# The mixers' output product: pair differences on GpSimd instead of VectorE, and the last pair's operands formed ahead of the first product

## The chip, the cores and the metric

The kernel runs on one core of one Trainium2 chip. The metric is the device time of one execution in microseconds (us), the median of several runs. TensorE multiplies matrices into PSUM banks, VectorE and ScalarE do element-wise work and read PSUM, GpSimd works on SBUF only and issues transfers of its own queue, SyncE issues the other transfers. Every engine works through its own instructions in the order of the program.

## The reference, cut to what matters

One decoder layer on 512 tokens with 1024 channels: a half-step FFN, two parallel mixers (a convolution module and a dilated attention), a gated sum of both through one output matrix, a second half-step FFN, a per-layer embedding and a last norm. The change touches the output of the mixers:

```python
a = jax.nn.silu(layer_norm(a, g_ln, b_ln))
y_conv = a @ w_conv_out                       # unit "co": 8 column blocks of 128
y_attn = o.reshape(b, s, ATTN_OUT_W) @ w_attn_out
g_a, g_b = jnp.split(jax.nn.sigmoid(gate_logits), 2, axis=-1)
h = h + (g_a * y_conv + g_b * y_attn) @ w_mix_out
h = h + 0.5 * swiglu(rms_norm(h, g_ffn2), w_ffn2_gate, w_ffn2_up, w_ffn2_down)
```

## The kernel before

Activations lie channel by token in tiles of 128x512 floats. Every float operand of a product is split into a high and a low half (a ScalarE copy in reduced precision makes the high one, a VectorE subtraction the low one), and a product is three matmuls: high by high, low by high, high by low.

The output matrix of the mixers is multiplied in a scheme with seven products instead of eight (`MIXED`: B11, T1, T2, B22, T3, B21, T4). Its eight input tiles are the gated sums `sg` of channel blocks 0 to 7. They form four pairs, block m with block m+4; each half is 256 tokens wide. `form_pair` queues the operands of a pair: differences of halves (`sub`, L638), ScalarE copies (`first_`, L650) and VectorE subtractions for the low halves (`end`, L653). Its parameter `by` names the engine of the differences. The two FFNs take the default (GpSimd); the mixers' output passes `BY`, which is VectorE before.

The stage that the change touches runs like this:

- The loop over m = 0 to 7 (L1519 on) runs `unit(p, ("co", m), cv)`, 24 matmuls of 128x512, then up to `N_FORM` = 10 queued steps of the pair of the turn before, then a multiplication by the gate (L1526, reads PSUM), the addition of the attention half (L1527), and the call of `form_pair` for this m. For m below 4 that queues five steps, one difference among them (T1's). For m from 4 on it queues ten: the difference t2, the copies for B21 with B22 and for T2, the low half of B21 with B22, two more differences, the low half of T2, the copy and the low half of T3 with T4, and a clean-up.
- So the ten steps of the last pair (m = 7, queued when the loop is over) are left for the products. `slab` fetches the weights of a product and, in the same call, prepares weights for products two or more ahead: a ScalarE copy (L401) and a VectorE subtraction (L402), each 128x1024, or weight sums on VectorE (L316 to L339), or the POOL transfers that form a low half by accumulation (L371, L373).
- In `for q in MIXED` (group g = 0, then g = 1) each product takes its slab, waits in the program for the operands that it needs, runs 24 matmuls of 128x256 in each half (`quarters_of`, L707, L708, L710), and `add` (L722, L725) adds the bank to the residual. Then `AFTER_M` says how many queued steps follow.
- B11, T2, T3 and T4 go to one PSUM bank (`pa`), T1 and B22 to `pd`, B21 to `pe`. A product accumulates on what its predecessor left in the bank, so the matmuls of T2 may start only when the addition of B11 has read `pa`, and those of B22 only when the addition of T1 has read `pd`.

On VectorE the order before is thus: gate and sum of block 7, the weight subtraction for T2, the addition of B11, t2, the low half of B21 with B22, the weight subtraction for B22, the addition of T1, two differences, the low half of T2.

Of the kernel before, what the change touches and what calls it, by code (L numbers as in the profile page):

```python
# [73 lines left out]

PLAN = (("gu", 2), ("gu", 3), ("gu", 4), ("gu", 5), ("dn", 1, 0), ("dn", 1, 1), ("gu", 6), ("gu", 7), ("gu", 8),
        ("dn", 2, 0), ("dn", 2, 1), ("gu", 9), ("gu", 10), ("dp", 0), ("dn", 3, 0), ("dn", 3, 1))
BY_ = False
N_FORM = 10
AFTER_M = {"B11": 4, "T1": 4, "T2": 3, "B22": 2, "T3": 2, "B21": 2, "T4": 2}
AFTER = {"B11": 1, "B21": 1, "T2": 1, "T1": 1, "T3": 2, "B22": 2}  # L80
TABLES = {"B21": 1, "T3": 1, "B22": 1, "T1": 1}
TABLES_P = 1
# [72 lines left out]
def block_kernel(ctx: ExitStack, tc: tile.TileContext, a, out):  # L155
# [208 lines left out]
    def spend(a_=0.0, v=0.0):  # L364
        spent[0] += a_
        spent[1] += v
# [242 lines left out]
    jobs, later = [], []  # L609
# [5 lines left out]
    def next_job(queue=None):  # L615
        f, a_, v = (queue or jobs or later).pop(0)
        if queue is not later:
            spend(a_, v)
        f()
# [368 lines left out]
    def into(v, xs, norm, resid):  # L988
        seen = []

        def first_(m):
            xs[m] = split(resid[m], "xs", gain(v, m))

        def second(m):
            norm.add(resid[m])
            seen.append(m)
            if len(seen) == KD:
                norm.flush()
        return first_, second
# [477 lines left out]
    def side(n):  # L1477
        if not bg:
            if lns:
                lns.pop(0)()  # L1480
        else:
            background(n)
# [33 lines left out]
    while lns:  # L1516
        side(0)
    BY = G if BY_ else V
    mixes, begun = [{} for _ in range(4)], []  # L1519
# [12 lines left out]
    begun = None  # L1532
    t = None
    cv.clear()
    xs, norm = [None] * KD, Norm()
    nxt2 = into(V_G2, xs, norm, h)
    for g in range(2):
        ps = {q: bank(q) for q in ("pa", "pe", "pd")}
        for q in MIXED:
# [8 lines left out]
            if g == 0:  # L1548
                for _ in range(min(AFTER_M.get(q, 0), len(later))):
                    next_job(later)  # L1550
# [4 lines left out]
            if g:  # L1555
                for _ in range(4 if q in ("B21", "T4") else min(AFTER_M.get(q, 0), len(later))):
                    next_job(later)
# [170 lines left out]
```

## Time and profile before

| | |
|---|---|
| median of 3 runs | 1286.78 us (1285.67 to 1287.22) |
| profiled execution, its own time | 1285.89 us |
| span of that execution | 1284.0 us |
| TensorE busy | 1269.0 us, 99% of the span |
| VectorE, ScalarE, GpSimd busy | 1017.2, 741.8, 300.8 us |
| granted TensorE clock | 0.998 of full speed, mean over the span |

A busy share tells little in so full a kernel. What matters is which engine TensorE waits for, and where; the rows of the section below show one stretch of some 30 us around the end of the loop over m, and the places elsewhere in the trace where GpSimd forms the same differences.

### The profile page before, as it was taken

To read this page: it belongs to the slowest core of one execution; us is meant where nothing else is said; L and a number is where in the kernel's file an instruction comes from. 1 tells how busy PE (TensorE), PEld (TensorE's weight loads), DVE (VectorE), ACT (ScalarE), POOL (GpSimd) and SP (SyncE) were. 2 spreads that over 40 slices of the span, in tenths; PEclk is the share of its full clock that TensorE was granted. 3 is DMA by queue.
4 is the path that set the end of the run, shared out by engine and by line. 5 is a ranking of instruction groups with operands and counts; after the bars stand their busy time and mean duration, and the time that the engine had idled before them with its cause. 6 is when DMAs were issued, how large, how long until landed. Compare 5 with 4: busy or idle time off the path is not lost.

```text
span 1284.0 us, 21810 instructions
## 1 busy us (share of the span) xinstructions
PE 1269.0 (99%) x8266; PEld 1163.2 (91%) x8266; DVE 1017.2 (79%) x1633; ACT 741.8 (58%) x1089; POOL 300.8 (23%) x392
## 2 busy tenths in 40 slices
PE   9999999999999999999999999999999999999997
PEld 7899999998988888989898888898999999998976
DVE  6988788898969887878778755876988878786865
ACT  6677566585633264746556345364777566584652
POOL 3122122132223232323322222012122122132000
PEclk9999999999999999999999999999999999999999
DMA  9676876867879889898887779557576876867541
GB/s 297 153 174 159 203 205 149 210 171 185 195 179 227 213 153 199 152 191 157 169 182 168 169 183 229 144 132 197 131 184 160 203 201 156 212 162 188 138 109 56
DMA packets 118224, 226.12 MB, mean 176 GB/s; under 512 B 20584, under 2 KB 54760, under 8 KB 118120
## 3 DMA queue, kind: packets, MB, share of 16 engines
q0 software_dynamic: 49600, 142.10, 54.8%
q1 hardware_dynamic: 68232, 82.37, 20.6%
q8 instruction: 65, 1.06, 0.3%
q14 instruction: 39, 0.32, 0.1%
q10 hardware_dynamic: 288, 0.26, 0.1%
HBM read 168.56 MB, written 2.13 MB: 133 GB/s over the span
## 4 chain that ended last, share of the span: by engine, by line
PE 72%; DVE 4%; DMA 1%; issue 1%; ACT 1%; POOL 0%; SPq 0%; ACTq 0%; DVEq 0%; POOLq 0%
PE pa L710 5%; PE pa L708 5%; PE pa L707 5%; PE pq L453 4%; PE pq L455 4%; PE pq L454 4%; PE pg L453 3%; PE pg L454 3%; PE pg L455 3%; PE pd L710 2%; PE pd L707 2%; PE pd L708 2%; PE pb L454 2%; PE pb L455 2%; PE pb L453 2%; PE pe L710 1%
## 5 line engine op out<-in xcount | busy, mean ns | idle before, releaser
L373 POOL DMA_DIRECT2D wl<-wr x108 | 93.4, 867 | 442.8 <-ACT wl L371 368.1
L707 PE MATMUL pa<-bh,wh 128*128 128x256 f32 x680 | 167.5, 283 | 0.6 <-DVE gx L722 0.4
L708 PE MATMUL pa<-bl,wh 128*128 128x256 f32 x680 | 167.2, 283 | 0.0
L1093 DVE SCALAR_TENSOR_TENSOR acc<-glu,taps,acc 128x511 f32<-128x511 f32 (+14 forms) x240 | 161.6, 732 | 0.0
L402 DVE TENSOR_TENSOR wl<-s,wh 128x1024 fp32r<-128x1024 f32 (+1 forms) x96 | 108.5, 1132 | 38.8 <-ACT wh L401 38.5
L371 ACT ACTIVATE wl<-wh 128x1024 fp32r<-128x1024 f32 x84 | 87.9, 1051 | 78.6 <-DMA wh<-in_w_in 55.5
L707 PEld LDWEIGHTS pa<-bh,wh 128*128 128x128 f32 x680 | 130.5, 192 | 1.0 <-issue 0.5
L708 PEld LDWEIGHTS pa<-bl,wh 128*128 128x128 f32 x680 | 130.5, 192 | 0.0
L371 ACT ACTIVATE wl<-wr 128x1024 fp32r<-128x1024 f32 (+1 forms) x108 | 105.7, 979 | 23.2 <-DVE wl L402 11.5
L401 ACT ACTIVATE wh<-s 128x1024 fp32r<-128x1024 f32 (+1 forms) x96 | 93.1, 969 | 37.8 <-PE pd L454 15.1
L385 ACT ACTIVATE wh<-wr 128x1024 fp32r<-128x1024 f32 (+1 forms) x108 | 105.5, 977 | 12.1 <-PE pd L710 6.1
L707 PE MATMUL pd<-bh,wh 128*128 128x256 f32 x448 | 110.2, 283 | 0.0
L708 PE MATMUL pd<-bl,wh 128*128 128x256 f32 x448 | 110.2, 283 | 0.0
L373 POOL DMA_DIRECT2D wl<-in_w_in x56 | 48.2, 864 | 219.5 <-ACT wl L371 200.4
L710 PE MATMUL pa<-bh,wl 128*128 128x256 f32 x680 | 96.9, 283 | 0.0
L453 PE MATMUL pq<-xsh,wh 128*128 128x512 f32 x224 | 88.7, 396 | 0.0
L710 PEld LDWEIGHTS pa<-bh,wl 128*128 128x128 f32 x680 | 88.4, 192 | 0.0
L454 PE MATMUL pq<-xsl,wh 128*128 128x512 f32 x224 | 87.3, 390 | 0.0
L455 PE MATMUL pq<-xsh,wl 128*128 128x512 f32 x224 | 87.3, 390 | 0.0
L707 PEld LDWEIGHTS pd<-bh,wh 128*128 128x128 f32 x448 | 86.0, 192 | 0.0
L708 PEld LDWEIGHTS pd<-bl,wh 128*128 128x128 f32 x448 | 86.0, 192 | 0.0
L453 PE MATMUL pg<-xsh,wh 128*128 128x512 f32 x192 | 76.2, 397 | 0.4 <-ACT xsh L473 0.4
(328 smaller groups left out, 3619.0 us busy)
## 6 DMA issues: line engine op xcount, KB each, us to landing
wl<-wr POOLq DMA_DIRECT2D x72, 512.0 KB, 5.8
wh<-in_w_in POOLq DMA_DIRECT2D x56, 512.0 KB, 7.1
wl<-in_w_in POOLq DMA_DIRECT2D x56, 512.0 KB, 6.3
wr<-in_w_ffn_up SPq DMA_DIRECT2D x80, 256.0 KB, 4.5
wr<-in_w_ffn_gate SPq DMA_DIRECT2D x78, 256.0 KB, 4.5
wr<-in_w_ffn_down SPq DMA_DIRECT2D x96, 192.0 KB, 3.8
wl<-wr POOLq DMA_DIRECT2D x36, 384.0 KB, 4.5
wr<-in_w_ffn_down SPq DMA_DIRECT2D x16, 256.0 KB, 4.3
```

What stands on the lines that cost most here:

```text
L371: A.activation(l.bitcast(F32R), h, AF.Copy, scale=-1.0)
L373: G.dma_start(to, src, accum_op=OP.add)
L385: A.activation(h, r, AF.Copy)
L401: A.activation(h, r, AF.Copy)
L402: V.tensor_sub(l, r, h.bitcast(F32))
L453: PE.matmul(ps, wh, xh, start=start, stop=False, skip_group_check=part)
L454: PE.matmul(ps, wh, xl, start=False, stop=False, skip_group_check=part)
L455: PE.matmul(ps, wl, xh, start=False, stop=stop, skip_group_check=part)
L707: PE.matmul(o, h[:, c], th, start=q in ("B11", "B21", "T1") and i == 0, stop=False, skip_group_check=True)
L708: PE.matmul(o, h[:, c], tl, start=False, stop=False, skip_group_check=True)
L710: PE.matmul(o, l[:, c], th, start=False, stop=i >= len(at) - 2, skip_group_check=True)
L1093: bg.append(lambda acc=acc, g=g, w=w, s=s: V.scalar_tensor_tensor(acc[:, s:], g[:, :S - s], w, acc[:, s:], op0=OP.mult, op1=OP.add))
```

## The change

Three constants and a loop. The differences of the mixers' pairs go to GpSimd (`BY_`). Seven of the last pair's ten steps are issued right behind the loop over m, before the slab of B11 is asked for (`N_FIRST`). Behind B11 no queued steps follow any more, behind T1 three instead of four; the same table serves g = 1, where the steps for the second FFN's inputs of blocks 4 and 5 so come one product later.

```diff
-BY_ = False
+BY_ = True
 N_FORM = 10
-AFTER_M = {"B11": 4, "T1": 4, "T2": 3, "B22": 2, "T3": 2, "B21": 2, "T4": 2}
+N_FIRST = 7
+AFTER_M = {"B11": 0, "T1": 3, "T2": 3, "B22": 2, "T3": 2, "B21": 2, "T4": 2}
@@ behind the loop over m
     cv.clear()
+    for _ in range(N_FIRST):
+        next_job(later)
     xs, norm = [None] * KD, Norm()
```

The differences of `form_pair` in the mixers' output (`by=BY`): one in each of the pairs of m = 0 to 3 (`t1`), three when the second block of a pair is there (`t2`, and two in `t34`), 16 in all.

## Rows read from the trace of the kernel before

**Rows 1.** Waits of TensorE, whole span: who waited for whom, total us, times, longest.
```profile
PE pa L708 <- DVE b L653: 1.9, 1, 1.9
...
PE pa L707 <- DVE gx L722: 0.4, 1, 0.4
```

**Rows 2.** TensorE in order of time: start us, length us, line, tiles, [idle before, releaser].
```profile
829.42 0.28 PE L707 MATMUL pa<-b,wh 128*128 128x256 f32 x1
...
835.17 0.28 PE L707 MATMUL pa<-b,wh 128*128 128x256 f32 x1
...
838.80 0.39 PE L708 MATMUL pa<-b,wh 128*128 128x256 f32 x1 [1.91 <-DVE b L653]
...
840.22 0.28 PE L707 MATMUL pd<-bh,wh 128*128 128x256 f32 x1
```

**Rows 3.** VectorE in order of time, around the first products.
```profile
831.53 0.69 DVE L1527 TENSOR_TENSOR sg<-sg,sg 128x512 f32<-128x512 f32 x1
832.14 1.22 DVE L402 TENSOR_TENSOR wl<-s,wh 128x1024 fp32r<-128x1024 f32 x1
833.28 0.75 DVE L725 SCALAR_TENSOR_TENSOR h<-pa,h 128x256 f32<-128x256 f32 x2
...
838.33 0.42 DVE L653 TENSOR_TENSOR b<-t,b 128x256 fp32r<-128x256 f32 x1
```

**Rows 4.** VectorE in order of time, turns m = 4 to 6 of the loop.
```profile
813.30 0.69 DVE L1526 TENSOR_TENSOR sg<-sg,py 128x512 f32<-128x512 f32 x1 [1.65 <-PE py L455]
...
819.48 0.69 DVE L1527 TENSOR_TENSOR sg<-sg,sg 128x512 f32<-128x512 f32 x1
820.09 1.22 DVE L320 TENSOR_TENSOR s<-wr,s 128x1024 f32<-128x1024 f32 x1
821.23 0.42 DVE L638 TENSOR_TENSOR t<-sg,t 128x256 f32<-128x256 f32 x1
821.56 0.69 DVE L653 TENSOR_TENSOR bl<-sg,bh 128x512 fp32r<-128x512 f32 x1
...
824.23 0.68 DVE L1526 TENSOR_TENSOR sg<-sg,py 128x512 f32<-128x512 f32 x1
```

**Rows 5.** GpSimd in order of time, second FFN, while VectorE has nothing running.
```profile
939.29 0.73 POOL L638 TENSOR_TENSOR t<-u 128x256 f32<-128x256 f32 x1 [5.57 <-DVE u L871]
940.10 0.74 POOL L638 TENSOR_TENSOR t<-u,t 128x256 f32<-128x256 f32 x1
```

**Rows 6.** VectorE and GpSimd in order of time, three differences behind one another.
```profile
1035.00 2.78 DVE L653 TENSOR_TENSOR b<-u,b 128x256 fp32r<-128x256 f32 x1
1035.08 1.03 POOL L638 TENSOR_TENSOR t<-u,t 128x256 f32<-128x256 f32 x1
1035.79 1.01 POOL L638 TENSOR_TENSOR t<-u 128x256 f32<-128x256 f32 x1
1036.48 1.00 POOL L638 TENSOR_TENSOR t<-u,t 128x256 f32<-128x256 f32 x1
```

**Rows 7.** VectorE and GpSimd in order of time, where VectorE came first.
```profile
1163.09 1.14 DVE L339 TENSOR_TENSOR s<-wr,wr 128x768 f32<-128x768 f32 x1 [2.08 <-DMA wr<-in_w_ffn_down]
1163.49 1.35 POOL L638 TENSOR_TENSOR t<-u,t 128x256 f32<-128x256 f32 x1
```

**Rows 8.** GpSimd in order of time: its transfers in the stage.
```profile
807.01 0.83 POOL L373 DMA_DIRECT2D wl<-in_w_conv_out  x1 [5.27 <-ACT wl L371]
812.44 0.85 POOL L373 DMA_DIRECT2D wl<-wr  x1 [4.60 <-ACT wl L371]
841.26 0.84 POOL L373 DMA_DIRECT2D wl<-wr  x1 [27.98 <-ACT wl L371]
```

**Rows 9.** ScalarE in order of time: the copy for T3 and T4 of one pair.
```profile
822.95 0.63 ACT L650 ACTIVATE bh<-t 128x512 fp32r<-128x512 f32 x1 [0.86 <-DVE t L638]
```

**Rows 10.** Stretches at the span's end: length, busy PE, PEld, DVE, ACT, POOL (instructions), clock, DMA.
```profile
1270.00:1275.00 5.00, 4.50 (x38) 4.30 (x37) 3.03 (x8) 2.67 (x7) 0.00 (x0) 1.00 0.29 107
1275.00:1280.00 5.00, 0.00 (x0) 0.00 (x0) 3.44 (x16) 1.30 (x5) 0.00 (x0) 0.89 0.00 0
```

## The prediction

> **What bounds the kernel now.** I read the list of TensorE's waits first, then the stretch in which the longest of them lies, engine by engine. TensorE is busy 99% of the span, so time is to be had only where it stands still. In the whole list there is one wait of some size: 1.9 us for the low half of an operand `b` [rows 1]. In order of time it lies in the third product of the mixers' output [rows 2]: B11 begins at 829.42, T2 at 835.17, two products later, so one takes 2.88 us. T2 should have been followed by B22 at 838.05; B22 begins at 840.22. The stall costs 2.17 us with its restart, and that is all that this change can give back: 0.17%.
>
> Why is `b` late? It is T2's operand from the last pair, and VectorE forms it at 838.33 [rows 3], some ten instructions after the gated sum of block 7 (831.53 to 832.22). The addition of B11, on which T2 waits too since it accumulates in the same bank, starts at 833.28 and is done at 834.03: 1.1 us ahead of need. That margin decides this case. TensorE does wait for such an addition where it is late; one of the other waits of the list is of that kind (0.4 us) [rows 1].
>
> **The change part by part.** *The move to GpSimd.* 16 differences of 128x256 leave VectorE, where one is 0.42 us long and holds its engine 0.33 us (821.23 to 821.56) [rows 4]. On GpSimd the same operation takes 0.73 us where VectorE is idle, begun 0.81 us apart when the second needs the first [rows 5]. Three in a row show 1.03, 1.01 and 1.00 us each, but begin 0.70 us apart [rows 6]: what counts in a series is 0.70. I take it, with 0.81 us as the upper end.
>
> What they do to VectorE is the larger question. A subtraction of two SBUF tiles that is 0.42 us long alone took 2.78 us when it met three GpSimd differences: it started at 1035.00 and ended at 1037.78, 0.30 us behind the last of them (1037.48) [rows 6]. In the other direction, a difference that started 0.40 us behind a weight sum took 1.35 us and ended 0.61 us behind it [rows 7]. So the two engines do such work in turn, not beside each other, and differences that are queued back to back are not interrupted. For VectorE a difference on GpSimd then costs 0.70 us instead of 0.33.
>
> The Trainium skill, SBUF — State Buffer, § Who interferes with whom, states the cause: a VectorE instruction with two SBUF inputs contends with a GpSimd one that reads SBUF, and the second to issue blocks until the first is done. That speaks against the change, and [rows 6] agree that it blocks, though not where that section makes the lock one instruction long; what that would change is a rival below.
>
> *The turns m = 0 to 3* have one difference each. It queues behind a transfer, the last at 807.01 [rows 8]: 0.83 for the transfer, 0.73 for the difference and, by estimate from the two 256-wide rows, 0.42 each for copy and low half make the next gate step (it follows the unit that ends near 807.9) some 1.5 us late. Ahead of the gate step of m = 4, at 813.30, VectorE idles 1.65 us [rows 4], and the weight sum and the next difference need 0.1 or 0.2 more. So m = 4 is on time or 0.1 us late.
>
> *The turns m = 5 to 7.* One turn on VectorE after the change is: weight sum 1.14 (820.09 to 821.23), three GpSimd differences 2.10, low half of B21 with B22 0.61 (512 wide, as the sum step), of T2 0.33, of T3 with T4 0.61, gate 0.72 (estimate: 0.68 long, and the next step needs its result), sum 0.61 (819.48 to 820.09) [rows 4, 6]. That is 6.1 us. Before, the gate steps of m = 4 and 6 lie 10.93 us apart [rows 4], 5.46 a turn, which is TensorE's pace. ScalarE's 0.63 us copy [rows 9] lies beside two low halves (0.94) and adds nothing. So VectorE, level with TensorE until now, falls back 0.65 us in each of m = 5 and 6. In turn 7 it has two weight steps, 1.14 more: 7.25 us. From the sum step of m = 4 at 814.1 the sum of block 7 begins at 814.1 + 12.2 + 7.25 = 833.55 and ends at 834.25, against 832.22 before.
>
> *The last pair directly behind the unit.* Seven steps now stand on VectorE's and ScalarE's queues ahead of T2's weight halves and of the addition of B11. GpSimd's queue is free (transfers at 812.44 and 841.26, none between) [rows 8], so t2 starts at 834.35 and the three differences last to 836.45. VectorE's low half of B21 with B22 waits for them, then 0.61, then T2's operand 0.33: ready at 837.4, 1.4 us sooner than before. But behind these stand the weight subtraction for T2, 1.14, and only then the addition of B11, 0.75 [rows 3]: 836.45 + 0.61 + 0.33 + 1.14 + 0.75 = 839.28, less some 0.1 us since each starts before the last one's end. **Who waits now is T2's first matmul**, at 839.2 instead of 835.17. B22 follows 2.88 us later at 842.1, against 840.22: **1.85 us more**. The wait for `b` is gone and a longer one, for the addition of B11, has taken its place.
>
> *What is moved besides.* ScalarE's copy of T2's weights (L401) goes behind the copy for T2's operand, to about 836, before VectorE wants it. The addition of T1 follows that of B11 by one weight step, at about 840.4 to 841.1, ahead of B22 at 842.1. The POOL transfer for B21 (841.26) waits for ScalarE, which is not later than TensorE's new pace. In g = 1 four steps move one product later with nothing waiting for them. I cost these at nothing; their cover is the 2 to 4 us by which TensorE itself is later, and without it each could cost its own half microsecond. Behind the stage TensorE has no wait near this size that could absorb it: the list goes from the longest down, and that is the 1.9 us [rows 1].
>
> **The sum.** The profiled execution took 1285.89 us, 1.89 over its span and 0.89 below the median of the runs. 1285.89 + 1.85 = 1287.7; against the median 1286.78 + 1.85 = **1288.6 us**, +0.14%. Ends: with 0.81 for 0.70 in the twelve differences of the last four pairs 1.3 more, 1289.9; with a difference as cheap for VectorE as its own 0.33, 0.37 times twelve or 4.4 less in VectorE's time, T2 then starting no sooner than 835.17, 2.17 below before: 1284.6. I stay near 0.70 since [rows 6] have the same three differences in the same order.
>
> **The rivals.**
>
> *GpSimd works beside VectorE* here, because the tiles or the order differ from those of [rows 6]. Then VectorE gains 0.33 in every difference and is back at TensorE's pace at m = 7; the sum of block 7 ends near 831, T2's operand is ready near 833.5, the addition of B11 at about 835.3, 0.2 behind T2's place: the 2.17 us come back but for 0.2, 1284.8. Against it: [rows 6, 7]. For it: VectorE waits for ScalarE or PSUM at times, when a difference is free for it (0.73 us alone) [rows 5]. Chance 0.22, with half-way cases to 1286.
>
> *VectorE gets in between two differences.* The low halves then run between the differences, the third one ends later, and the 0.63 us copy [rows 9] is no longer hidden: 0.6 us more in each of three turns, 1.8, less the 0.7 by which the addition of B11 may pass the third difference of the last pair: 1.1 on top of the forecast, 1289.7. Against it: the VectorE instruction of [rows 6] waited through all three. Chance 0.10. (The lock of one instruction, as the Trainium skill has it in SBUF — State Buffer, § Who interferes with whom, would be this case.)
>
> *The clock falls: the slower end.* By the forecast TensorE stands still for some 4.1 us (835.1 to 839.2). At the end of the span the matmuls stop near 1274.5, and the stretch 1275 to 1280 has a mean grant of 0.89 [rows 10]: full speed, then half for 0.11 / 0.5 of 5 us, 1.1 us, so the grant fell at 1278.9, 4.4 us after the last matmul. A stall as long as that would put T2 at half speed (1.2 instead of 2.4 GHz): up to 2.88 us more, and half of it if the grant comes back midway. It decides from a stall of about 4.4 us; the forecast is 0.3 below. 1285.9 + 0.9 + 1.85 + 2.2 = 1290.8 against the median. The 1.9 us stall of before left the clock alone. Chance 0.13.
>
> **How the numbers follow.** The forecast (VectorE and GpSimd in turn, addition of B11 last, 1287.2 to 1289.9) has 0.55; the rivals 0.22, 0.10, 0.13. 0.2%, which is 2.57 us, is about what a measurement of this kernel can tell from no change. Faster by that would be below 1284.2, more than the whole stall: 0.02. Slower, above 1289.35: the clock 0.13, half of the second rival 0.05, the upper end of the forecast 0.08, in all 0.26. Within: 0.72. The range for 8 in 10 goes from 1285.0, which leaves out the full gain, to 1291.0.
>
> **What would show it.** Right: no wait of TensorE for `b`, one of 3 to 5 us for the addition L725 ahead of T2; the loop's low halves (L653) in m = 5 to 7 lasting 2 us and more instead of 0.69, each behind three POOL rows; the sum of block 7 near 833.5 instead of 831.5. Wrong: low halves of 0.69 us beside POOL rows and T2 at 835.2 (first rival); POOL rows of line 638 with VectorE's in between (second); a clock below 1.00 in the stretch around 840 (third). What would upset all of it: a transfer of the convolution weights that the GpSimd differences hold up, so that a unit of the loop starts late.

## The result, and the profile after

The changed kernel takes 1290.03 us (median, 1288.77 to 1290.66), the kernel before beside it 1286.54 us. The ratio is 1.0025 with a 95% interval of 1.0017 to 1.0032: slower by about 3.2 us (the two medians lie 3.49 apart). The forecast was 1288.6, 1.85 above the median it was set against; sign and place were right, the size was little more than half of what came. The profiled execution took 1290.05 us with a span of 1288.2. Lines of the changed kernel are numbered one to three higher than before (L725 is L726, L653 is L654, L638 is L639).

The waits of TensorE after the change (who for whom, total us, times, longest), to hold against [rows 1]:

```profile
PE pa L708 <- DVE h L726: 4.7, 1, 4.7
...
PE pa L708 <- DVE gx L723: 0.4, 1, 0.4
```

The wait for `b` is gone. In its place stands one for the addition of B11 (`h`, L726), two and a half times as long. TensorE in order of time (start, length), to hold against [rows 2]:

```profile
829.60 0.28 PE L708 MATMUL pa<-b,wh 128*128 128x256 f32 x1
...
840.24 0.47 PE L708 MATMUL pa<-b,wh 128*128 128x256 f32 x1 [4.73 <-DVE h L726]
...
844.69 0.28 PE L708 MATMUL pd<-bh,wh 128*128 128x256 f32 x1
```

The first line is B11's first matmul: B11 begins at 829.60. T2 begins at 840.24 instead of 835.17. And T2, 24 matmuls that take 2.88 us, lasts until 844.69, 4.45 us. Why it is slow is in the stretches (length, busy PE, PEld, DVE, ACT, POOL, granted clock, DMA):

```profile
839.00:840.00 1.00, 0.00 (x0) 0.00 (x0) 1.00 (x3) 1.00 (x3) 0.00 (x0) 1.00 0.00 0
840.00:841.00 1.00, 0.76 (x4) 0.79 (x5) 1.00 (x2) 1.00 (x3) 0.00 (x0) 0.66 0.00 0
841.00:842.00 1.00, 1.00 (x6) 1.00 (x6) 1.00 (x4) 0.96 (x2) 0.69 (x1) 0.50 0.00 0
842.00:843.00 1.00, 1.00 (x6) 1.00 (x6) 1.00 (x2) 0.00 (x0) 0.16 (x1) 0.50 0.34 66
843.00:844.00 1.00, 1.00 (x8) 1.00 (x7) 0.63 (x1) 0.07 (x1) 0.00 (x0) 0.63 1.02 197
```

The column behind POOL's is the grant: 1.00 until 840, 0.50 from 841 to 843. TensorE had done nothing since 835.5 or so, its clock fell to 1.2 GHz just as T2 began, and the grant was back at full speed in the stretch from 844 on.

VectorE in order of time, to hold against [rows 4] for the turn and against [rows 3] for what stands ahead of T2:

```profile
814.55 0.69 DVE L1528 TENSOR_TENSOR sg<-sg,sg 128x512 f32<-128x512 f32 x1
815.16 1.22 DVE L317 TENSOR_TENSOR s<-s,wr 128x1024 f32<-128x1024 f32 x1
816.30 1.23 DVE L654 TENSOR_TENSOR bl<-sg,bh 128x512 fp32r<-128x512 f32 x1
817.46 0.94 DVE L654 TENSOR_TENSOR b<-t,b 128x256 fp32r<-128x256 f32 x1
819.70 0.69 DVE L654 TENSOR_TENSOR bl<-t,bh 128x512 fp32r<-128x512 f32 x1 [1.29 <-ACT bh L651]
820.31 0.68 DVE L1527 TENSOR_TENSOR sg<-sg,py 128x512 f32<-128x512 f32 x1
821.02 0.69 DVE L1528 TENSOR_TENSOR sg<-sg,sg 128x512 f32<-128x512 f32 x1
...
834.76 0.69 DVE L1528 TENSOR_TENSOR sg<-sg,sg 128x512 f32<-128x512 f32 x1
836.21 0.69 DVE L654 TENSOR_TENSOR bl<-sg,bh 128x512 fp32r<-128x512 f32 x1 [0.76 <-ACT bh L651]
836.82 0.95 DVE L654 TENSOR_TENSOR b<-t,b 128x256 fp32r<-128x256 f32 x1
837.69 1.74 DVE L403 TENSOR_TENSOR wl<-s,wh 128x1024 fp32r<-128x1024 f32 x1
839.35 0.74 DVE L726 SCALAR_TENSOR_TENSOR h<-pa,h 128x256 f32<-128x256 f32 x2
```

One turn, sum to sum, takes 6.47 us (814.55 to 821.02) against TensorE's 5.44. The low halves that took 0.69 and 0.42 us now take 1.23 and 0.94, and the last one waits 1.29 us for ScalarE's copy. The sum of block 7 begins at 834.76 instead of 831.53, and the addition of B11 at 839.35 instead of 833.28. GpSimd in the same turn (the first line is a transfer, the next three are the differences), and the first difference of the last pair:

```profile
814.71 0.86 POOL L374 DMA_DIRECT2D wl<-wr  x1 [1.70 <-ACT wl L372]
815.40 1.57 POOL L639 TENSOR_TENSOR t<-sg,t 128x256 f32<-128x256 f32 x1
816.94 1.18 POOL L639 TENSOR_TENSOR t<-sg,sg 128x256 f32<-128x256 f32 x1
818.08 0.92 POOL L639 TENSOR_TENSOR t<-sg,t 128x256 f32<-128x256 f32 x1
...
835.53 0.72 POOL L639 TENSOR_TENSOR t<-sg,t 128x256 f32<-128x256 f32 x1 [2.79 <-DVE sg L1528]
```

The same operation takes 0.72 us where VectorE is idle and 1.57 beside the weight sum. Both engines lose when they meet. They take turns one instruction at a time: the first difference ends (816.97) behind the weight sum, the low half (816.30 to 817.53) behind the first difference, the second difference (818.12) behind the low half. It is not a matter of a tile that both use: the weight subtraction at 837.69 reads neither `sg` nor `t`, and beside the last of the differences it takes 1.74 us instead of 1.22.

### The profile page after: what moved, and what is told of

It is laid out like the page before. It is cut to its first block, busy times and chain, and to the rows that moved or that the text cites. A ratio compares the mean times of both kernels' runs of the same rounds, so it can differ in the third digit from the quotient of the medians.

```text
span 1288.2 us, 21816 instructions
## 1 busy us (share of the span) xinstructions
PE 1269.9 (99%) x8266; PEld 1163.9 (90%) x8266; DVE 1017.0 (79%) x1617; ACT 741.9 (58%) x1089; POOL 318.9 (25%) x408
## 4 chain that ended last, share of the span: by engine, by line
PE 65%; issue 6%; DVE 3%; POOL 3%; DMA 1%; ACT 1%; SPq 0%; ACTq 0%; POOLq 0%; DVEq 0%
PE pa L708 5%; PE pa L709 5%; PE pa L711 5%; PE pq L454 4%; PE pq L455 4%; PE pq L456 4%; PE pd L711 2%; PE pd L709 2%; PE pd L708 2%; PE pg L454 2%; PE pg L456 2%; PE pg L455 2%; PE pg L1602 1%; PE pe L709 1%; PE pe L711 1%
```

## The experiments

To compare kernels I use the time from the start of B11 to the start of B22, which does not change when the whole trace is shifted, and beside it the measured ratio to the kernel before with its interval. From 1 us of difference, 0.0008 in the ratio would follow.

| kernel | B11 to B22, us | T2 waits, us | ratio |
|---|---|---|---|
| before | 10.80 | 1.9, in its middle | |
| changed | 15.09 | 4.7 | 1.0025 (1.0017 to 1.0032) |
| changed, again | 15.72 | 4.6 | 1.0027 (1.0016 to 1.0037) |
| GpSimd only | 13.00 | 1.9 and 2.0 | 1.0017 (1.0009 to 1.0026) |
| order only | 10.16 | 1.3 | 0.9992 (0.9983 to 1.0001) |
| seven behind B11 | 8.63 | none | 0.9977 (0.9968 to 0.9985), 0.9979 (0.9970 to 0.9988) |
| seven behind B11, GpSimd | 11.57 | 1.8 and 0.2 | 0.9998 (0.9989 to 1.0007) |
| idle differences | 14.62 | 3.9 and 0.4 | 1.0029 (1.0019 to 1.0039) |
| idle writes | 8.63 | none | 0.9986 (0.9977 to 0.9995) |
| stand filled, 28 | 13.65 and 15.49 | 1.4 and 1.8 | 1.0023 (1.0014 to 1.0032), twice |
| stand filled, 38 | 13.50 | none | 1.0019 (1.0010 to 1.0028) |

**The two halves of the change, each alone.** First only the engine; it is read against the kernel before:

```diff
-BY_ = False
+BY_ = True
```

> Only the differences move to GpSimd; the last pair's steps stay behind the products as before. Theory (GpSimd and VectorE do two-input SBUF work in turn): the turns of the loop are as late as in the changed kernel, the sum of block 7 begins near 834.8 instead of 831.5, the addition of B11 ends near 838.3, T2 starts there instead of at 835.2, and T2 waits a second time for the last pair's operand; neither stand is as long as 4.4 us, so the clock stays. B22 begins near 842.8 against 840.2: 2.6 us more than before, ratio 1.0020. Rival (GpSimd works beside VectorE, the new order alone costs): the sum of block 7 at 831.0 or sooner, ratio 1.0000 or below.

The stage's waits in that kernel:

```profile
PE pa L708 <- DVE b L653: 2.0, 1, 2.0
PE pa L707 <- DVE h L725: 1.9, 1, 1.9
```

The old wait is still there, and the new one has come on top. The sum of block 7 begins at 834.83, as expected; the addition of B11 ends at 837.33, 1 us sooner than expected, and B22 begins at 842.63. The expected 2.6 us are 2.2, and the ratio, 1.0017, is clear of 1.

Then only the order, with the differences on VectorE:

```diff
+N_FIRST = 7
-AFTER_M = {"B11": 4, "T1": 4, ...}
+AFTER_M = {"B11": 0, "T1": 3, ...}
 (and the loop over N_FIRST, as in the change)
```

> Only the order changes: seven steps of the last pair directly behind the loop, the differences still on VectorE. Theory: the sum of block 7 begins at 831.5 as before, the seven steps and the weight subtraction push the addition of B11 from 834.0 to an end near 836.5, T2 starts at 836.5 instead of 835.2 and doesn't stop in its middle; B22 begins near 839.4 against 840.2: 0.8 us less than before, ratio 0.9994. Rival (the new order is the cause of the loss): T2 starts near 840, ratio 1.002 or more.

```profile
834.73 1.22 DVE L403 TENSOR_TENSOR wl<-s,wh 128x1024 fp32r<-128x1024 f32 x1
835.87 0.75 DVE L726 SCALAR_TENSOR_TENSOR h<-pa,h 128x256 f32<-128x256 f32 x2
```

This is VectorE ahead of T2: the addition of B11 ends at 836.62, as expected, and T2, which stands 1.3 us, starts 0.14 us behind it. (The list of waits names a ScalarE copy of weights here, but that was done at 835.3.) The order alone is a gain of 0.64 us in the stage; it exchanges the wait for the operand for a shorter one for the addition. Its ratio, 0.9992, can't be told from 1. So the engine is what made the changed kernel slower, and the order made the engine's price felt in one piece: 2.2 and -0.6 alone, 4.3 together. Of these 4.3, 1.57 are T2 at the lower clock, and 2.7 are waiting.

**The order that the prediction's margin suggests.** If the addition of B11 has 1.1 us to spare and the operand none, the seven steps belong behind that addition, ahead of the next weight step:

```diff
-AFTER_M = {"B11": 4, "T1": 4, ...}
+AFTER_M = {"B11": 7, "T1": 3, ...}
```

> The differences stay on VectorE, and the seven steps go behind the addition of B11 (AFTER_M 7 for B11, 3 for T1, nothing ahead of the products). Theory: the addition of B11 keeps its place at 833.3 to 834.0, the last pair's operand for T2 is ready near 836.1, before T2 comes to it at 836.9; the addition of T1 ends near 837.8, before B22's place at 838.05. No wait of TensorE in the stage: 2.0 us less than before, ratio 0.9984. Rival (the addition of T1 becomes the next late one): T2 without a stop but B22 waiting, 1 us less, ratio 0.9992.

```profile
835.48 0.28 PE L707 MATMUL pa<-b,wh 128*128 128x256 f32 x1
838.36 0.28 PE L707 MATMUL pd<-bh,wh 128*128 128x256 f32 x1
```

T2 (first line) runs 2.88 us to B22 without a stop, and the list of TensorE's waits has no line of this stage. 1283.38 us: faster than both kernels. The 2.17 us of the stall came back whole, and the median moved by 3.2. Whether the 1 us between the two is chance, a second comparison of the same kernel was to tell.

> The kernel with seven steps behind the addition of B11 and the differences on VectorE, once more on this chip: no wait of TensorE in the stage, ratio 0.9977 (0.9968 to 0.9985 the first time), mean clock 0.998 in most runs. If the 0.9 us beyond the 2.2 us of the stall were chance: 0.9983.

1283.62 us, ratio 0.9979. The larger gain came again, but both intervals, 0.9968 to 0.9985 and 0.9970 to 0.9988, still hold the 0.9983 that the stall alone would give. So whether there is more to gain than the stall is not settled; what speaks for it stands in the last section.

**The same order, with GpSimd.**

```diff
 (as the one before)
-BY_ = False
+BY_ = True
```

> The order of the best kernel so far (seven steps behind the addition of B11, three behind T1's), but the differences on GpSimd. Theory (two-input work in turn): the turns of the loop are as late as in the changed kernel, the sum of block 7 begins near 834.8, the addition of B11 ends near 837.3, T2 starts there, 1.9 us late, B22 waits for the addition of T1 until some 841.3: 0.9 us more than before and 3 more than with the differences on VectorE, ratio 1.0007. Rival (with the additions in the right place the engine of the differences doesn't matter): ratio 0.9977.

```profile
837.32 1.24 DVE L653 TENSOR_TENSOR bl<-sg,bh 128x512 fp32r<-128x512 f32 x1
838.48 0.96 DVE L653 TENSOR_TENSOR b<-t,b 128x256 fp32r<-128x256 f32 x1
```

T2 starts at 837.54 and B22 at 841.38, as expected; these two steps, VectorE's low halves for the last pair, are again 1.24 and 0.96 us long. The engine of the differences alone is worth 11.57 - 8.63 = 2.9 us in this order, and the medians of the two kernels on one chip, 1286.58 and 1283.62 us, say the same. (The ratio to the kernel before, 0.9998, came out below the 1.0007 expected.)

**Is it contention, or only a slower producer?** VectorE waits for results of the differences, too. To take that away, the next kernel leaves the differences on VectorE and lets GpSimd form three more for each pair of m = 4 to 7, which nobody reads:

```diff
 (in the best order; GpSimd behind t2)
+scr = T("scr")[:, lo]
+for _ in range(3):
+    G.tensor_sub(scr, x2[:, hi], x2[:, lo])
```

> The kernel with seven steps behind the addition of B11 (differences on VectorE), and with each pair of m = 4 to 7 GpSimd forms three differences of 128x256 into a tile that nobody reads. Nothing waits for them. Theory (two-input SBUF work of GpSimd and VectorE goes in turn): each turn of VectorE is some 2.1 us longer than its 5.0, against 5.44 of TensorE; the sum of block 7 begins near 836 instead of 831.8, T2 starts near 838.3 and stops once more for its operand; B22 near 842.3 against 838.4: 3 to 4 us more than without them, ratio 1.0010 against the kernel before. Rival (they work beside each other, and the loss in the changed kernel is that its VectorE waits for results of a slower engine): no change, ratio 0.9977.

```profile
815.41 3.68 POOL L674 TENSOR_TENSOR scr<-sg 128x256 f32<-128x256 f32 x3 [1.51 <-DVE sg L1536]
816.37 0.96 DVE L638 TENSOR_TENSOR t<-sg,t 128x256 f32<-128x256 f32 x1
817.26 1.23 DVE L653 TENSOR_TENSOR bl<-sg,bh 128x512 fp32r<-128x512 f32 x1
```

T2 and B22 of that kernel:

```profile
839.80 0.36 PE L716 MATMUL pa<-b,wh 128*128 128x256 f32 x1 [3.86 <-DVE h L734]
...
844.65 0.33 PE L716 MATMUL pd<-bh,wh 128*128 128x256 f32 x1
```

VectorE's own difference takes 0.96 us and its low half 1.23, though they wait for nothing of GpSimd's. Work that nobody needs costs 14.62 - 8.63 = 6.0 us in the stage, where 3 to 4 were expected. The turn of VectorE is the expected 7.1 us, but T2 comes 1.5 us later than expected, and the clock fell in it. That fall is some 0.5 of the 6.0, by an estimate: from T2's second stop to B22 it took 1.92 us (842.73 to 844.65), in the kernel before 1.42 (838.80 to 840.22). The rest is contention.

The counterpart keeps GpSimd busy with writes of a constant; only a one-column copy ahead of them reads SBUF:

```diff
+G.tensor_copy(scr[:, :1], x2[:, :1])
+for _ in range(6):
+    G.memset(scr, 0.0)
```

> As the one with idle differences, but GpSimd fills the unused tile with a constant six times (128x256 each) behind a one-column copy that ties it to the sum of the block: GpSimd is as busy or nearly so and writes SBUF, but reads none. Theory (what excludes the other is reading: VectorE's second SBUF input): VectorE's low halves keep 0.69 us beside it, no wait ahead of T2, ratio 0.9977 to 0.9985. Rival (any GpSimd work on SBUF blocks VectorE): low halves of 1 us and more, sum of block 7 late by 2 us and more, ratio 1.000 or above.

```profile
816.46 2.16 POOL L676 MEMSET scr<- 128x256 f32 x6
816.61 0.69 DVE L654 TENSOR_TENSOR bl<-sg,bh 128x512 fp32r<-128x512 f32 x1
817.21 0.42 DVE L639 TENSOR_TENSOR t<-sg,sg 128x256 f32<-128x256 f32 x1
```

Beside 2.16 us of writes the low half keeps its 0.69 us and the difference its 0.42; B11 to B22 is 8.63 us, as without any GpSimd work. The ratio, 0.9986, is about 1 us above those of the kernel without the writes; the intervals overlap, and no wait in the stage goes with it. What holds up VectorE's instructions with two SBUF inputs is thus GpSimd's reading and not its writing. The reading tested is that of subtractions with two inputs; GpSimd work with one input of full size was not tried.

**What the fall of the clock cost.** The changed kernel, with matmuls into an unused bank between T1 and T2 of the first group, whose result is left unused:

```diff
+if g == 0 and q == "T1":
+    f = bank("fill")
+    for _ in range(28):
+        PE.matmul(f[:, :256], wh[:, :P], mixes[0]["T1"][0], start=True, stop=True)
```

> The changed kernel with 28 matmuls of 128x256 into an unused PSUM bank between T1 and T2 of the first group; their result is used by nobody. They take some 3 us of a stand that is 4.7 us long without them. Theory (4.5 us of loss are 2.9 of waiting and 1.6 of a clock that fell during the stand): T2 starts at the same 840.2, the clock stays at 1.00, T2 takes 2.88 us instead of 4.45: 1.6 us less than the changed kernel, some 1.9 us more than before, ratio 1.0015. Rival (the recorded fall of the clock costs nothing, or T2 is slow for another reason): T2 still takes 4.4 us, ratio 1.0025 or more.

In that profile the clock held and B11 to B22 fell from 15.09 to 13.65 us. But the ratio, 1.0023, cannot be told from the changed kernel's. Both once more on one chip:

> The changed kernel once more, unaltered, on the same chip as the filled one, since their first intervals (1.0017 to 1.0032 and 1.0014 to 1.0032) come from different chips and overlap. Theory (the fall of the clock costs 1.5 us): ratio 1.0030, 1.2 to 1.6 us above the filled kernel. Rival (the fall costs nothing): equal to the filled kernel.

> The changed kernel with 28 unused matmuls in the stand ahead of T2, once more, beside the unaltered one. Theory: clock 1.00 in the stage, T2 2.95 us long; ratio 1.0018. Rival: the same as the unaltered one, 1.0028.

The changed kernel's T2 and B22, then the filled one's (filling, T2, B22):

```profile
840.08 0.55 PE L708 MATMUL pa<-b,wh 128*128 128x256 f32 x1 [4.57 <-DVE h L726]
...
845.32 0.28 PE L708 MATMUL pd<-bh,wh 128*128 128x256 f32 x1
```

In this second profile the grant fell while TensorE still stood, as two stretches of the changed kernel show (the grant is 1.00 until 838):

```profile
838.00:839.00 1.00, 0.00 (x0) 0.00 (x0) 1.00 (x1) 1.00 (x3) 0.18 (x1) 0.72 0.02 8
839.00:840.00 1.00, 0.00 (x0) 0.00 (x0) 1.00 (x4) 1.00 (x2) 0.00 (x0) 0.50 0.00 0
```

The filled kernel:

```profile
835.77 3.52 PE L1554 MATMUL fill<-b,wh 128*128 128x256 f32 x28
841.08 0.36 PE L709 MATMUL pa<-b,wh 128*128 128x256 f32 x1 [1.79 <-DVE h L727]
...
843.16 0.41 PE L710 MATMUL pa<-b,wh 128*128 128x256 f32 x1
...
845.51 0.28 PE L709 MATMUL pd<-bh,wh 128*128 128x256 f32 x1
```

In the changed kernel T2 took 5.24 us here. In the filled one, too, the clock fell this time, though TensorE stood for only 1.79 us: T2's matmuls are 0.41 us long instead of 0.28, and it took 4.43 us. So 28 were no clean remedy, and the comparison of these two settles nothing. With 38:

> The changed kernel with 38 unused matmuls in the stand ahead of T2 instead of 28, some 4.8 us at 0.126 each, so that TensorE is idle there for less than half a microsecond. With 28 it was idle 1.4 us in one profile, where the clock held, and 1.8 in another, where it fell just behind the stand. Theory: the clock holds, T2 takes 2.9 us, B22 begins near 843.3 instead of 844.7 to 845.3: ratio 1.0017, with a mean clock of 0.998 in most runs. Rival (the fall of the clock is not what made T2 long): T2 4.4 us, ratio 1.0027.

```profile
835.14 4.72 PE L1554 MATMUL fill<-b,wh 128*128 128x256 f32 x38
839.94 0.36 PE L709 MATMUL pa<-b,wh 128*128 128x256 f32 x1
842.89 0.28 PE L709 MATMUL pd<-bh,wh 128*128 128x256 f32 x1
```

TensorE now stands for almost nothing, T2 starts where it did and takes 2.95 us. Against these 2.95 us, the fall costs 1.5 and 2.3 us in the two traces of the changed kernel, out of 4.3 and 4.9 in all. The mean grant of the span points the same way in every run: 0.994 to 0.996 in all 18 runs of the changed kernel, 0.997 or 0.998 in all 11 with 38. The medians agree in direction (1.0019 against 1.0025 and 1.0027, about 0.9 us), but their intervals overlap.

## Why the prediction was right, and where it fell short

- *What can be gained.* Right: 2.17 us in the stage, and the kernel with the seven steps behind the addition of B11 got just that there.
- *The two engines do two-input work in turn.* Right, and shown apart from any waiting for results by the idle differences (6.0 us, some 0.5 of it the clock) and the idle writes (none).
- *GpSimd keeps its turn through a series of three.* Wrong here. This was read off [rows 6], and the kernel followed the rival that I gave 0.10: VectorE gets in between two differences, and no low half in the loop lasted the 2 us that I had named as the sign of being right. The third difference then ends later and the copy for T3 and T4 is no longer hidden (the 1.29 us wait for ScalarE). The term that was mis-sized is the turn: 6.1 us forecast, 6.47 measured, in both m = 5 and 6; turn 7 was 7.27 for a forecast of 7.25. The rival had its price wrong, too: 0.6 us more a turn, for 0.37, 0.37 and 0.02. With turns 0 to 3 and m = 4 somewhat later than forecast (0.5 us instead of 0.1; 0.2 of that is in the whole trace), the sum of block 7 came at 834.76 instead of 833.55. The Trainium skill, SBUF — State Buffer, § Who interferes with whom, has the lock one instruction long, and in this stage it was; the rule was nearer than my row.
- *Who waits.* Right: T2's first matmul for the addition of B11, and no longer for `b`. Forecast for T2: 839.2; measured 840.24. From the sum's end to the addition's end it took 4.64 us (835.45 to 840.09), for 4.95 forecast.
- *The clock.* Its fall was a rival with a chance of 0.13, on the condition of a stall of some 4.4 us, the 4.4 read off [rows 10]; the forecast stand was 4.1. The stand became 4.7 us for the reason above, and the clock fell in both profiles of the changed kernel. But the 4.4 was one reading, and no bound. In the second profile TensorE stopped at 835.5 and the grant fell near 838.4 (by the 0.72 of that stretch), some 3 us into the stand; with the idle differences it fell behind a stand of 3.9 us. So the forecast stand of 4.1 us was not safely below it, and the chance was set too low. T2 took 4.45 and 5.24 us for 2.88.
- *The sum.* Forecast: 1.85 us more. Measured in the profile, B11 to B22: 4.29 us more, of which 1.57 are the clock and 2.72 the waiting, where 1.85 was forecast. Of this, the medians show 3.2 to 3.5 us; why they differ is not shown, and an inference stands below. The 1290.03 us lie just above the forecast's own 1287.2 to 1289.9 and inside the range for 8 in 10, which ends at 1291.0. They came there by the second and the third rival together, which I had as separate cases with 0.10 and 0.13, and both of their signs were seen: VectorE between the rows of the differences, and a clock below 1.00 around 840. Sign, place and what TensorE waits for are owed to the reckoning; that the time fell into the range is in part luck.
- *What is moved besides.* Right as far as shown: no other wait of TensorE above 0.6 us behind the start of the span.

## What to carry to other kernels

Work on GpSimd that reads SBUF is not free for VectorE: two-input instructions of both went in turn here, and a difference that cost VectorE 0.33 us cost it 0.5 to 0.7 on the other engine (0.69 to 1.23 us for a low half in the loop; 0.70 a difference in [rows 6]). Before steps are moved ahead of an instruction, look at who waits for what stands behind them on the same engine: here the addition that frees a PSUM bank had 1.1 us to spare and the operand none, and seven steps behind that addition, rather than in front of it, gave all of the stall back. And a stand can cost more than its length, when the clock falls in it or just behind it.

## What the runs showed of the hardware that I had not expected

**The order of turns between GpSimd and VectorE differs from place to place.** In [rows 6] one VectorE instruction waited through three differences (2.78 us); in the loop of the changed kernel, and with the idle differences, the engines changed after every instruction (1.23 and 0.94 us). The series of [rows 6] comes directly behind a transfer of GpSimd's (at 1034.47), but so does that of the turn shown above (at 814.71), and there they changed after every instruction. So a transfer ahead does not decide it; what does is not tested.

**The clock can fall in a shorter stand than I thought, or just behind it.** It fell some 3 us into a stand in the second profile of the changed kernel, behind a stand of 3.9 us with the idle differences (0.73 in the stretch from 840 to 841, T2 from 839.80), and in the second profile of the filled kernel behind a stand of 1.8 us that followed 28 matmuls. In the first profile of the filled kernel, behind 1.4 us, and with GpSimd only, behind two stands of 1.9 and 2.0 us, it held. So the length of the stand alone does not decide it. In the stretches of the filled kernel's second profile the grant is 1.00 during the stand and falls only when T2 has begun:

```profile
840.00:841.00 1.00, 0.00 (x0) 0.00 (x0) 1.00 (x4) 1.00 (x2) 0.00 (x0) 1.00 0.00 0
841.00:842.00 1.00, 0.92 (x6) 0.95 (x7) 1.00 (x2) 0.83 (x1) 0.00 (x0) 0.79 0.00 0
842.00:844.00 2.00, 2.00 (x11) 2.00 (x11) 2.00 (x5) 1.90 (x2) 0.85 (x1) 0.50 0.35 68
```

**The 1.9 us stall of the kernel before may already cost clock in some of its runs.** Of 86 runs of it beside the experiments, 34 had a mean grant of 0.998 and took 1285.9 us in the mean, 35 had 0.997 and took 1287.0, 17 had 0.996 and took 1287.5. The best kernel, which has no stall there, had 0.998 in 18 of 22 runs, at 1283.7. Against the runs of before at 0.998 its gain is 2.2 us, the stall's 2.17; against the mean of all 86 it is 3.0. So the rest of its gain, and the 1 us by which the changed kernel's medians lie nearer to those of before than its trace, would fit a clock that falls in a part of the runs of before. That is an inference and not shown: the one trace of before has the clock at full speed in this stage, and no trace of a run at 0.996 was taken. Nor is 0.997 a sign of such a fall by itself: the second profile of the best kernel has that mean with a grant of 1.00 in every stretch up to 1270 us, and falls only at the end of the span.
